# Eight small reorderings in one fused pair of transformer blocks: later side work, halves moved between transposings, loads behind a loop, tiles by k

## The chip, the cores and the metric

One core of one Trainium2 chip runs the whole program. The metric is the device time of one execution in microseconds (us), lower is better. The engines are TensorE (PE, its weight loads PEld), VectorE (DVE), ScalarE (ACT), GpSimd (POOL) and SyncE (SP), which here only issues DMA loads.

## What is computed

A hybrid block (layer norm, a gated delta rule beside stick-breaking attention, gates, an output projection, a mixture of experts) and then a second block of two layers (attention with rotary positions and a squared-ReLU MLP, then a pooling mixer and another MLP). 256 tokens plus 16 meta tokens, width 1024, all tensors float32. Cut to what matters:

```python
proj = h @ w_in                                     # 1024 -> qkv, z, beta, alpha, sb_qkv, gates
o_dn = gated_delta_rule_chunked(l2_normalize(q) * 128 ** -0.5, l2_normalize(k), v, beta, g)
o_dn = rms_norm(o_dn, dn_norm_g) * silu(dn_z)
o_sb = stick_breaking_attention(sq, sk, sv)
merged = gate0 * (o_dn @ w_branch_dn) + gate1 * (o_sb @ w_branch_sb)
h = layer_norm(alpha * h + merged @ w_out)
ffn = hierarchical_moe(h)                           # 4 groups x 8 experts, 2 experts per token
x = layer_norm(alpha * h + ffn)
...
x = x + moba_attention(rms_norm_2(x), w_qkv, w_o, cos, sin)
x = x + squared_relu_mlp(rms_norm_2(x), w_up, w_down)
x = x + pool_mixer(rms_norm_2(x), w_groups, ls_scale)
x = x + squared_relu_mlp(rms_norm_2(x), w_up, w_down)
return rms_norm_2(x, norm_final)
```

## The kernel before, in words

**Halves.** Dense weights come in chunks of 1 MB (`wraw`), two halves of 128x1024 each. ACT casts a half to a rounded high part (L324), DVE subtracts that from the original to get the low part (L326, tile `wsplit`), and PE does three matmuls per product: high by high, low by high, high by low (L374, L375, L376 in `ws_half`, L412 to L414 in `xs_half`). So a half costs 24 matmuls of 256 columns or 12 of 512, and it can't go on without DVE's subtract. Halves are prepared ahead in four slots, and five raw chunks fit the ring. In the wide form (`ws_wide`, L385 and L386) tokens are split too, and one 512-column and one 256-column matmul per k does it.

**Order.** The kernel is written engine by engine through a framework that schedules each engine's queue when the program is built. `tc.issue_after(x)` puts an instruction behind `x` in its queue's order, without a wait. `wpost.after = (a, b)` does that to the cast (a) and the subtract (b) of the next halves of the second block's stream. Every engine runs its queue strictly in that order.

**Stages**, with the lines that the change touches:

- *First block's middle.* Three generators are stepped in turn: the delta rule (`delta`, its matrix inversions step by step, and a reciprocal root `rq` of the query norms, L811 and L812, made of the ten small DVE operations L437 to L446), the projections, and two stick-breaking attentions (L909 to L940). In the round with `it == 2` `router_weights` (L994 to L998) scales the router's matrix.
- *Branches.* For each of two token tiles c, DVE multiplies `oraw` by a gate (L1069) and PE transposes it (L1072). `BS_AT` says which of the four halves of the second branch's matrix run behind which transposing: (0, 1, 1) is one half behind c = 0, none behind c = 1, and three at the end. L957 evacuates them.
- *Experts.* 99 chunks of 1 MB (`wexp`) stream through; PE multiplies 32-row groups (L1460 is the down product). In the last group a loop `For_i` over overflowing experts runs `n_x` times, which is zero times here, but every engine passes its ends (L1551). Behind it stand the last down product, its scaling (`ysf`, L1555 on ACT, L1556 on DVE) and eight adding matmuls (L1559). The loop's spare weights use one buffer that `slot()` gives, and two loads of the second block (`wraw`) are issued by SP ahead of the loop. Then 32 filler matmuls (L507) run until the layer norm (L470, L471, L1578 to L1585) is through and PE transposes `h` (L1610); ACT and DVE make the tokens `xx` of the second block (L1614, L1616).
- *Second block's projections.* Six column groups n, each in four halves k0 = 0, 2, 4, 6; the first two run as `xs_front` (L424). POOL sums the squares (L1636, L1644, L1646) and `rstd_columns` has PE sum them over partitions (L1659) at n = 0, k0 = 6. `rope_rows` scales a group's rows (L1690), turns them (L1696), and PE transposes them (L1705) at k0 = 2 of the next group.
- *MLPs.* Four products of up tiles per group through `ws_wide`, then down (L1831 to L1833). The tokens come one k at a time (L1597, L1598).
- *Pool mixer.* The last down product feeds `last`: per token tile c a root (L454 to L461 on DVE) scales the pooling matrix, on DVE for c = 0 (L1893), on ACT for c = 1 (L1891). PE multiplies by it (L1908, then L1910 and L1911), and the result meets the mixer's weights.

Of the kernel before, what the change touches and what calls it, by code (L numbers as in the profile page):

```python
# [19 lines left out]
SEQ = 256  # L20
# [4 lines left out]
NG = 8  # L25
CAP = 32
LATE = 8
RS_AT = 6
FILL_SPEC = "0123"
# [19 lines left out]
G_ELSE = (1, 4, 6)  # L49
BS_AT = (0, 1, 1)  # L50
COUNT_AT = 0
DN_STEPS = (3, 5, 10, 11, 11)
DN_FILL = (7, 9)
# [229 lines left out]
def tile_hybrid_block(ctx: ExitStack, tc: tile.TileContext, A, out, dump=None, stop=99):  # L283
# [95 lines left out]
    def ws_wide(stream, m, xx, fn, newbank):  # L379
# [7 lines left out]
        fn(m, p)  # L387

    def ws_front(stream, ms, xh, xl, width, fn, newbank):

# [13 lines left out]
    def xs_half(stream, k0, nk, xh, xl, banks, t0=0):  # L404

        wh, wl = stream.half()
        for k in (k0, k0 + 1):
            w1 = wh[:, (k - k0) * 512:(k - k0 + 1) * 512]
            w2 = wl[:, (k - k0) * 512:(k - k0 + 1) * 512]
            for c in range(2):  # L410
                tsl = slice(t0 + c * 128, t0 + c * 128 + 128)
                PE.matmul(banks[c], xh[:, k, tsl], w1, start=k == 0, stop=False)  # L412
                PE.matmul(banks[c], xh[:, k, tsl], w2, start=False, stop=False)  # L413
                PE.matmul(banks[c], xl[:, k, tsl], w1, start=False, stop=k == nk - 1)  # L414

# [273 lines left out]
    def delta():  # L689
# [120 lines left out]
        V.tensor_scalar(rq, pn[:, :8], 1e-6, None, op0=OP.add)  # L810
        rq = rsqrt(rq, (128, 8))  # L811
        V.tensor_scalar(rq, rq, float(128.0 ** -0.5), None, op0=OP.mult)  # L812

# [13 lines left out]
        XTs = [None] * 3  # L827
        live = [0, 1, 2]
        while live:
            for i in list(live):  # L830
                r = next(gens[i])
                if r is not None:
                    XTs[i] = r
                    live.remove(i)
            yield
# [216 lines left out]
    while m_on or f_on or sticks:  # L1052
        if it == 2:
            router_weights()
# [342 lines left out]
    def overflow(wx):  # L1397
# [4 lines left out]
        def weights(i):  # L1402
            t = wx[:, i % 2 * 1024:i % 2 * 1024 + 1024]
            spare_weights(t, eg, ej, 2 * i, 2)
            return t
# [35 lines left out]
    def scatter(g, n, Pm, ys):  # L1441

        for c in range(2):
            for i in range(2):
                added[0] = PE.matmul(ya[c][n], Pm[:, c * 128:(c + 1) * 128], ys[i], start=g == 0 and i == 0,
                                     stop=g == NG - 1 and i == 1)

# [20 lines left out]
    for g in range(NG):  # L1468
# [72 lines left out]
        else:  # L1541
# [5 lines left out]

            wx = slot()
            with tc.issue_after(last_load[0].ins):
# [3 lines left out]
            down(py, full, hT, chunk(), 1)  # L1553
            ys = moe.tile([128, 512], F32, tag="xt", name="ysf")
            mark["ACT"] = S.activation(ys[:, :256], py[:, :256], AF.Copy, scale=Pw)  # L1555
            V.tensor_scalar(ys[:, 256:], py[:, 256:], Pw, None, op0=OP.mult)  # L1556
            for c in range(2):
                for q in range(2):
                    added[0] = PE.matmul(ya[c][1][:, hf[q]], Pm[:, c * 128:(c + 1) * 128].bitcast(F32), ys[:, hf[q]],  # L1559
                                         start=False, stop=q == 1)  # L1560
# [200 lines left out]
    for n in range(6):  # L1761
        pb = [bank2(), bank2()]
        for k0 in range(0, 8, 2):
            if n or k0 > 2:
                xs_half(wpost, k0, 8, xh, xl, pb)
            elif k0 == 2:
                xs_front(wpost, 2, 8, xh, xl, pb)
            if n == 0 and k0 == RS_AT:
                rs[:] = rstd_columns(acc)
            if k0 == 2:  # L1770
                for f in later:
                    f()
                later = []
            heads(n, k0)
        if n < 4:
            later.append(rope_rows(n, pb))
# [26 lines left out]
    def mlp(xx, acc, n_last, after):  # L1803
# [5 lines left out]
        def up(g):  # L1809
# [14 lines left out]

            for m in range(4):
                ws_wide(wpost, m, xx, fn, bank2)
# [59 lines left out]
    def last(c, n, o):  # L1886
        square_sum(c, n, o, ss)
        if n:
# [3 lines left out]
            else:  # L1892
                V.tensor_scalar(pmat[:, :, :144], pmat[:, :, :144], r, None, op0=OP.mult)  # L1893

# [32 lines left out]
    for q in range(2):  # L1927
        wh, wl = wpost.half()
        for j in range(4):
            m = 4 * q + j  # L1930
# [54 lines left out]
```

## Time and profile before

| | before |
|---|---|
| median of 3 runs | 1011.24 us (1010.31 to 1011.78) |
| the profiled execution's own time | 1012.06 us |
| its span | 1010.3 us |
| mean granted TensorE clock | 0.979 |
| busy PE, DVE, ACT, POOL | 944.3, 603.7, 483.4, 68.3 us |
| read from memory | 225.29 MB |

A row of the timeline gives start, duration, engine, line, operation, out<-in, shapes and count, and in brackets how long the engine was idle just before and what released it. Matmuls are pipelined, so a matmul's duration is longer than the distance to the next start; costs of many are taken by that distance. In a table by stretches "PEclk" is the granted clock: 1.00 is 2.4 GHz, 0.50 is 1.2 GHz, and numbers between mean that both occurred in the stretch.

### The profile page before, as it was taken

The page shows a single profiled execution, that of the slowest core. Times are in us where ns is not written, and L with a number is a line of the kernel's source. Part 1 is how long each engine was busy: PE and PEld are TensorE (multiplying, and loading weights), DVE is VectorE, ACT ScalarE, POOL GpSimd, SP SyncE. Part 2 cuts the span into 40 slices and gives each one's busy share as a digit, 9 for nine tenths or more (in the row PEclk, how much of TensorE's full clock was granted, in tenths as well). Part 3 has the DMA queues.
Part 4 walks back from the last instruction along what each step waited for, and adds up shares of the span by engine and source line. Part 5 has one row for each costly group of instructions (what it writes and reads, how often), then busy time and mean ns, then how long its engine had stood idle before and what let it go on. Part 6 is the DMA issues. An engine that isn't in the chain of part 4 may idle for free.

```text
span 1010.3 us, 14882 instructions
## 1 busy us (share of the span) xinstructions
PE 944.3 (93%) x5905; PEld 757.5 (75%) x5905; DVE 603.7 (60%) x1163; ACT 483.4 (48%) x846; POOL 68.3 (7%) x60
## 2 busy tenths in 40 slices
PE   6997999989999999987789999999999999999996
PEld 5996997989884534442368889888888788888885
DVE  7887564664863312231186777756666686666664
ACT  4855576434432111101155565755555576555552
POOL 0004232000300000000020001000000020000002
PEclk9999999999999999999989999999999999999999
DMA  9440223649689999999865434555555525555521
GB/s 363 165 165 1 90 84 121 249 187 355 249 315 406 416 425 423 426 423 426 352 236 179 167 126 176 180 174 201 180 195 182 193 84 209 184 191 182 193 84 42
DMA packets 34231, 227.32 MB, mean 225 GB/s; under 512 B 3936, under 2 KB 4704, under 8 KB 7664
## 3 DMA queue, kind: packets, MB, share of 16 engines
q1 hardware_dynamic: 34160, 226.36, 58.8%
q8 instruction: 47, 0.77, 0.3%
q14 instruction: 24, 0.20, 0.1%
HBM read 225.29 MB, written 1.05 MB: 224 GB/s over the span
## 4 chain that ended last, share of the span: by engine, by line
PE 72%; DMA 16%; DVE 6%; ACT 3%; POOL 2%; issue 1%; SPq 0%; POOLq 0%; ACTq 0%; DVEq 0%
DMA wexp<-in_wexp_dram 14%; PE bank L385 11%; PE bank L386 6%; PE acc L1831 6%; PE acc L1832 6%; PE acc L1833 6%; PE bank L375 5%; PE bank L376 5%; PE bank L374 5%; PE bank L413 3%; PE bank L414 3%; PE bank L412 3%; DMA wraw<-in_wpost_dram 2%; PE bank L1486 1%; DVE wsplit L326 1%; PE bank L674 1%
## 5 line engine op out<-in xcount | busy, mean ns | idle before, releaser
L326 DVE TENSOR_TENSOR wsplit<-wraw,wsplit 128x1024 fp32r<-128x1024 f32 x222 | 277.7, 1251 | 143.5 <-ACT wsplit L324 139.5
L324 ACT CAST wsplit<-wraw 128x1024 fp32r<-128x1024 f32 x222 | 233.0, 1051 | 144.8 <-PE acc L1833 79.7
L385 PE MATMUL bank<-xx,wsplit 128*128 128x512 f32 x512 | 179.0, 393 | 2.2 <-DVE xx L1598 2.2
L386 PE MATMUL bank<-xx,wsplit 128*128 128x256 f32 x512 | 142.8, 280 | 0.7 <-DVE wsplit L326 0.7
L385 PEld LDWEIGHTS bank<-xx,wsplit 128*128 128x128 f32 x512 | 96.1, 188 | 24.4 <-DVE xx L1598 3.5
L1831 PE MATMUL acc<-wsplit,mhh 128*128 128x512 f32 x256 | 100.5, 393 | 0.0
L1832 PE MATMUL acc<-wsplit,mhh 128*128 128x512 f32 x256 | 99.8, 390 | 0.0
L1833 PE MATMUL acc<-wsplit,mhl 128*128 128x512 f32 x256 | 99.7, 390 | 0.0
L386 PEld LDWEIGHTS bank<-xx,wsplit 128*128 128x128 f32 x512 | 96.2, 188 | 1.6 <-DVE wsplit L326 1.0
L375 PE MATMUL bank<-hh,wsplit 128*128 128x256 f32 (+1 forms) x304 | 88.4, 291 | 2.7 <-DVE wsplit L326 2.7
L374 PE MATMUL bank<-hh,wsplit 128*128 128x256 f32 (+1 forms) x304 | 89.6, 295 | 0.0
L376 PE MATMUL bank<-hl,wsplit 128*128 128x256 f32 (+1 forms) x304 | 87.7, 289 | 0.0
L1486 PE MATMUL bank<-wexp,xt 128*32 128x512 f32 x512 | 62.8, 599 | 5.3 <-DMA wexp<-in_wexp_dram 4.3
L375 PEld LDWEIGHTS bank<-hh,wsplit 128*128 128x128 f32 x304 | 58.6, 193 | 3.6 <-DVE wsplit L326 3.2
L374 PEld LDWEIGHTS bank<-hh,wsplit 128*128 128x128 f32 x304 | 58.7, 193 | 0.4 <-issue 0.2
L376 PEld LDWEIGHTS bank<-hl,wsplit 128*128 128x128 f32 x304 | 58.7, 193 | 0.0
L1833 PEld LDWEIGHTS acc<-wsplit,mhl 128*128 128x128 f32 x256 | 48.1, 188 | 10.1
L1832 PEld LDWEIGHTS acc<-wsplit,mhh 128*128 128x128 f32 x256 | 48.1, 188 | 9.9 <-DVE wsplit L326 0.3
L1831 PEld LDWEIGHTS acc<-wsplit,mhh 128*128 128x128 f32 x256 | 48.1, 188 | 9.7
L1816 ACT COPY relu<-bank 128x256 f32<-128x256 f32 x64 | 23.8, 373 | 62.8 <-PE bank L386 62.7
L1512 ACT ACTIVATE hid<-bank 128x256 f32<-128x256 f32 x8 | 3.1, 383 | 89.1 <-PE bank L1486 89.1
L1460 PE MATMUL bank<-wexp,hT 128*32 128x512 f32 x256 | 32.6, 624 | 9.8 <-DMA wexp<-in_wexp_dram 4.2
(542 smaller groups left out, 1648.8 us busy)
## 6 DMA issues: line engine op xcount, KB each, us to landing
wexp<-in_wexp_dram SPq DMA_DIRECT2D x99, 1024.0 KB, 19.6
wraw<-in_wpost_dram SPq DMA_DIRECT2D x81, 1024.0 KB, 4.7
wraw<-in_wpre_dram SPq DMA_DIRECT2D x30, 1024.0 KB, 4.9
h<-in_x_dram SPq DMA_DIRECT2D x2, 512.0 KB, 4.4
eb<-in_rowv_dram SPq DMA_DIRECT2D x2, 512.0 KB, 10.7
out_dram<-of SPq DMA_DIRECT2D x4, 256.0 KB, 2.1
cpre<-in_cst_dram SPq DMA_DIRECT2D x1, 915.5 KB, 10.3
pmat<-in_poolm_dram SPq DMA_DIRECT2D x1, 544.0 KB, 3.2
```

Source lines behind the costliest of these rows:

```text
L324: S.copy(hi, src)
L326: (sub or V).tensor_tensor(lo, src, hi.bitcast(F32), op=OP.subtract)
L374: PE.matmul(p[:, :width], wh[:, o:o + 128], xh[:, k, :], start=k == 0, stop=False)
L375: PE.matmul(p[:, :width], wl[:, o:o + 128], xh[:, k, :], start=False, stop=False)
L376: PE.matmul(p[:, :width], wh[:, o:o + 128], xl[:, k, :], start=False, stop=k == nk - 1)
L385: PE.matmul(p, wh[:, o], xx[:, k].rearrange("p q t -> p (q t)"), start=k == 0, stop=False)
L386: PE.matmul(p[:, :SEQ], wl[:, o], xx[:, k, 0], start=False, stop=k == 7)
L1460: behind[0] = PE.matmul(py[32 * e:32 * e + 32, sl], hT[:, i, 32 * e:32 * e + 32], w[:, e, sl], start=i == 0, stop=i == 1).ins
L1486: behind[0] = PE.matmul(pg[32 * e:32 * e + 32, :], xt[:, k, 32 * e:32 * e + 32], w[:, e, :], start=k == 0, stop=k == 7).ins
L1831: PE.matmul(ac[c][n], hh_, wh, start=g == 0 and k == 0, stop=False)
L1832: PE.matmul(ac[c][n], hh_, wl, start=False, stop=False)
L1833: PE.matmul(ac[c][n], hl_, wh, start=False, stop=g == 7 and k == 3)
```

## The change

The root `rq` is computed in the fourth round of the inversions, behind a mark in DVE's queue, and the router's weights in round 7. `BS_AT` becomes (0, 3, 3): three halves between the two transposings, one behind. The overflow loop takes its buffers from the weight ring, and the scaled rows behind the loop get two tiles, each for its own half; one 128x1 matmul per token tile closes the first half of the sums. The sums of squares are taken by PE at n = 1, behind the first half of that group, the first group's rotation comes after it, and its transposings at k0 = 4. The first two up tiles of both MLPs run by k, each k for both tiles (`wide_front`). The pooling matrix's first scaling becomes the mark behind which the subtracts of the next halves are put. Lines below line 50 move up by 1 to 26 numbers in the changed file (L326 becomes L327, L1893 L1918).

```diff
-RS_AT = 6
...
-BS_AT = (0, 1, 1)
+BS_AT = (0, 3, 3)
+ROUTER_AT = 7
+RQ_AT = 4
...
+    def wide_front(stream, ms, xx, fn, newbank):
+        ws = [stream.half() for _ in ms]
+        ps_ = [newbank() for _ in ms]
+        for k in range(8):
+            o = slice(k * 128, k * 128 + 128)
+            for (wh, wl), p in zip(ws, ps_):
+                PE.matmul(p, wh[:, o], xx[:, k].rearrange("p q t -> p (q t)"), start=k == 0, stop=False)
+                PE.matmul(p[:, :SEQ], wl[:, o], xx[:, k, 0], start=False, stop=k == 7)
+        for m, p in zip(ms, ps_):
+            fn(m, p)
...
-        rq = rsqrt(rq, (128, 8))
-        V.tensor_scalar(rq, rq, float(128.0 ** -0.5), None, op0=OP.mult)
...
         while live:
+            n_live += 1
+            if n_live == RQ_AT:
+                with tc.issue_after(mark["DVE"].ins):
+                    rq = rsqrt(rq, (128, 8))
+                    V.tensor_scalar(rq, rq, float(128.0 ** -0.5), None, op0=OP.mult)
...
-        if it == 2:
+        if it == ROUTER_AT:
             router_weights()
...
-            wx = slot()
+            wx = [ring.tile([128, 2048], F32, tag="w", name="wexp") for _ in range(N_RING)]
...
-            ys = moe.tile([128, 512], F32, tag="xt", name="ysf")
-            mark["ACT"] = S.activation(ys[:, :256], py[:, :256], AF.Copy, scale=Pw)
-            V.tensor_scalar(ys[:, 256:], py[:, 256:], Pw, None, op0=OP.mult)
+            ys = [moe.tile([128, 256], F32, tag="hT", name="ysf"), moe.tile([128, 256], F32, tag="xt", name="ysf")]
+            V.tensor_scalar(ys[0], py[:, :256], Pw, None, op0=OP.mult)
+            mark["ACT"] = S.activation(ys[1], py[:, 256:], AF.Copy, scale=Pw)
             for c in range(2):
+                PE.matmul(ya[c][0][:, 0:1], ident, C("strict")[:, 0:1], start=False, stop=True)
...
-            if n == 0 and k0 == RS_AT:
-                rs[:] = rstd_columns(acc)
-            if k0 == 2:
+            if n == 1 and k0 == 0:
+                with tc.issue_after(last_of[0].ins):
+                    rs[:] = rstd_columns(acc)
+                later.append(rope_rows(0, first_pb))
+            if k0 == (4 if n == 1 else 2):
...
-            for m in range(4):
+            if g == 0:
+                wide_front(wpost, (0, 1), xx, fn, bank2)
+            for m in range(2 if g == 0 else 0, 4):
                 ws_wide(wpost, m, xx, fn, bank2)
...
-                V.tensor_scalar(pmat[:, :, :144], pmat[:, :, :144], r, None, op0=OP.mult)
+                wpost.after = (None, V.tensor_scalar(pmat[:, :, :144], pmat[:, :, :144], r, None, op0=OP.mult))
```

Three places in the queues. First DVE's queue in the first block's middle, before, up to the subtract (L326) of the half that the projections use next; L927 are the stick-breaking scans, `rs_t` and `rs_y` belong to the root `rq`, `rcb` and `wrt` to the router's weights:

```order
L927 SCALAR_TENSOR_TENSOR sbwork<-sbwork 128x272
L443 TENSOR_TENSOR rs_t<-rs_t,rq 128x8
L995 TENSOR_REDUCE rcb<-bank 128x36
L444 TENSOR_SCALAR rs_y<-rs_t 128x8
L996 TENSOR_SCALAR rcb<-rcb 128x36
L997 TENSOR_TENSOR rcb<-rcb,cpre 128x36
L445 TENSOR_TENSOR rs_y<-rs_y,rs_t 128x8
L998 TENSOR_TENSOR wrt<-wr_1111,rcb 128x288
L446 SCALAR_TENSOR_TENSOR rs_y<-rs_y,rs_z 128x8
L326 TENSOR_TENSOR wsplit<-wraw,wsplit 128x1024
```

and changed, from the scan of 832 columns (L923, now L941), with which the same piece begins, on:

```order
L941 SCALAR_TENSOR_TENSOR sbwork<-sbwork 128x832
L327 TENSOR_TENSOR wsplit<-wraw,wsplit 128x1024
L945 SCALAR_TENSOR_TENSOR sbwork<-sbwork 128x144
L945 SCALAR_TENSOR_TENSOR sbwork<-sbwork 128x272
L945 SCALAR_TENSOR_TENSOR sbwork<-sbwork 128x144
L945 SCALAR_TENSOR_TENSOR sbwork<-sbwork 128x272
L327 TENSOR_TENSOR wsplit<-wraw,wsplit 128x1024
L958 COPY sbwork<-bank 16x512
L327 TENSOR_TENSOR wsplit<-wraw,wsplit 128x1024
L936 SCALAR_TENSOR_TENSOR sbwork<-bank,cpre 128x416 x2
```

That subtract (now L327) stands ahead of the four scans; the root and the router's tiles are gone from here.

Second, PE's queue in the second block's projections, before, at the sum over partitions (L1659). `wsplit_4716` is the fourth half of group 0, `wsplit_4781` the first of group 1:

```order
L412 MATMUL bank_4741<-wsplit_4716,xx_4660 128x512
L412 MATMUL bank_4742<-wsplit_4716,xx_4660 128x512
L1659 MATMUL bank_4800<-cst_73,acc1_4798 128x1 x2
L412 MATMUL bank_4847<-wsplit_4781,xx_4660 128x512
L413 MATMUL bank_4741<-wsplit_4716,xx_4660 128x512
L414 MATMUL bank_4741<-wsplit_4716,xx_4660 128x512
L413 MATMUL bank_4742<-wsplit_4716,xx_4660 128x512
```

and changed, where `wsplit_4723` and `wsplit_4788` are those two halves, and the sum over partitions (L1678 now) follows 22 matmuls behind the first two rows:

```order
L425 MATMUL bank_4748<-wsplit_4723,xx_4667 128x512
L425 MATMUL bank_4749<-wsplit_4723,xx_4667 128x512
L425 MATMUL bank_4803<-wsplit_4788,xx_4667 128x512
L426 MATMUL bank_4803<-wsplit_4788,xx_4667 128x512
L427 MATMUL bank_4803<-wsplit_4788,xx_4667 128x512
L425 MATMUL bank_4804<-wsplit_4788,xx_4667 128x512
L426 MATMUL bank_4804<-wsplit_4788,xx_4667 128x512
L426 MATMUL bank_4748<-wsplit_4723,xx_4667 128x512
L427 MATMUL bank_4748<-wsplit_4723,xx_4667 128x512
```

The sum is gone from the place behind the first two matmuls of the fourth half, and five matmuls of the next group stand there, ahead of the first one (L426) that reads the fourth half's low part.

Third, DVE's queue at the pooling matrix, before, from its scaling for c = 0 (L1893) to the end of the root for c = 1 (L461), which ACT's scaling waits for:

```order
L1893 TENSOR_SCALAR pmat<-pmat,r_7205 128x4x144
L456 SCALAR_TENSOR_TENSOR r_7240<-r_7238,rst 128x1
L457 SCALAR_TENSOR_TENSOR r_7239<-r_7240,r_7238 128x1
L458 SCALAR_TENSOR_TENSOR r_7240<-r_7239,rst 128x1
L459 TENSOR_SCALAR r_7238<-r_7240 128x1
L460 TENSOR_TENSOR r_7238<-r_7238,r_7240 128x1
L461 SCALAR_TENSOR_TENSOR r_7238<-r_7238,r_7239 128x1
L326 TENSOR_TENSOR wsplit<-wraw,wsplit 128x1024
```

and changed, the same piece (L1918 to L476):

```order
L1918 TENSOR_SCALAR pmat<-pmat,r_7212 128x4x144
L471 SCALAR_TENSOR_TENSOR r_7247<-r_7245,rst 128x1
L327 TENSOR_TENSOR wsplit<-wraw,wsplit 128x1024
L472 SCALAR_TENSOR_TENSOR r_7246<-r_7247,r_7245 128x1
L473 SCALAR_TENSOR_TENSOR r_7247<-r_7246,rst 128x1
L327 TENSOR_TENSOR wsplit<-wraw,wsplit 128x1024
L474 TENSOR_SCALAR r_7245<-r_7247 128x1
L475 TENSOR_TENSOR r_7245<-r_7245,r_7247 128x1
L476 SCALAR_TENSOR_TENSOR r_7245<-r_7245,r_7246 128x1
```

Two subtracts stand inside the root for c = 1: one stood behind it, the other far ahead of it, in front of the piece shown.

SP's queue loses the two `wraw` loads ahead of the loop and has all six behind it; the load of `causal` (192 KB, L1682), which stood behind those, is ahead of the loop now.

## Rows read from the trace of the kernel before

**Rows 1.** The page: shares of the chain that ended last, by engine

```profile
PE 72%; DMA 16%; DVE 6%; ACT 3%; POOL 2%; issue 1%; SPq 0%; POOLq 0%; ACTq 0%; DVEq 0%
```

**Rows 2.** Stretches: PE, PEld, DVE, ACT, POOL busy, PEclk, DMA share, GB/s

```profile
101.00:104.00 3.00, 3.00 (x13) 3.00 (x14) 1.25 (x3) 0.00 (x0) 0.00 (x0) 0.50 0.64 224
105.00:210.00 105.00, 102.78 (x822) 93.89 (x821) 64.81 (x105) 61.94 (x106) 22.70 (x13) 1.00 0.36 131
217.00:220.00 3.00, 2.61 (x13) 2.64 (x14) 0.94 (x2) 0.59 (x1) 0.00 (x0) 0.50 0.99 421
227.00:303.00 76.00, 73.73 (x512) 66.63 (x511) 47.62 (x112) 31.32 (x45) 8.65 (x8) 0.98 0.80 307
303.00:499.00 196.00, 176.83 (x1238) 80.50 (x1237) 50.60 (x139) 31.23 (x64) 0.00 (x0) 0.98 1.01 420
500.00:507.00 7.00, 5.12 (x16) 4.40 (x17) 3.23 (x8) 1.99 (x2) 0.00 (x0) 0.51 0.61 226
524.00:530.00 6.00, 4.77 (x13) 3.99 (x14) 4.91 (x17) 0.00 (x0) 1.17 (x1) 0.50 0.73 269
808.00:812.00 4.00, 3.50 (x30) 3.45 (x31) 2.65 (x8) 2.84 (x5) 0.00 (x0) 1.00 0.02 2
```

**Rows 3.** Timeline of DVE, first block's middle

```profile
99.68 1.21 DVE L326 TENSOR_TENSOR wsplit<-wraw,wsplit 128x1024 fp32r<-128x1024 f32 x1
```

**Rows 4.** Timeline of PE at the router's matmuls and its longest wait

```profile
85.33 1.13 PE L994 MATMUL bank<-wr,cst 128*128 128x288 f32 x4
...
89.61 0.63 PE L652 MATMUL bank<-cst,XT 128*128 128x128 f32 x4 [2.51 <-DVE XT L656]
```

**Rows 5.** Timeline of PE, the half that waits

```profile
96.53 0.37 PE L374 MATMUL bank<-hh,wsplit 128*128 128x272 f32 x1
...
100.95 0.59 PE L375 MATMUL bank<-hh,wsplit 128*128 128x272 f32 x1 [2.06 <-DVE wsplit L326]
...
105.37 0.38 PE L936 MATMUL bank<-cst,sbwork 128*128 128x128 f32 x2
```

**Rows 6.** Timeline of PE between the last transposings and behind

```profile
209.07 0.60 PE L1072 MATMUL bank<-cst,oraw 128*128 128x128 f32 x4
...
217.39 1.09 PE L1072 MATMUL bank<-cst,oraw 128*128 128x128 f32 x4 [4.87 <-DVE oraw L1069]
...
227.69 0.28 PE L374 MATMUL bank<-hh,wsplit 128*128 128x256 f32 x1
```

**Rows 7.** Chain of waits around the loop: start, us, what

```profile
481.12 20.29 DMA wraw<-in_wpost_dram
...
501.88 3.78 PE acc L1559 x8
...
510.57 0.57 ACT xx L1614
```

**Rows 8.** The page: the second block's loads, us from issue to landing

```profile
wraw<-in_wpost_dram SPq DMA_DIRECT2D x81, 1024.0 KB, 4.7
```

**Rows 9.** Timeline, all engines, projections of the second block

```profile
519.76 1.21 DVE L326 TENSOR_TENSOR wsplit<-wraw,wsplit 128x1024 fp32r<-128x1024 f32 x1
...
522.18 1.33 POOL L1644 TENSOR_TENSOR acc<-acc,sq 128x512 f32<-128x512 f32 x1
522.31 3.94 DVE L326 TENSOR_TENSOR wsplit<-wraw,wsplit 128x1024 fp32r<-128x1024 f32 x2
...
525.23 1.01 PE L1659 MATMUL bank<-cst,acc 128*128 128x1 f32 x4 [3.73 <-POOL acc L1646]
```

**Rows 10.** Waits of PE, projections to first layer's end

```profile
PE bank L385 <- DVE xx L1598: 0.9, 1, 0.9
```

**Rows 11.** Waits of PE, pool mixer and last MLP's start

```profile
PE bank L385 <- DVE xx L1598: 1.4, 3, 0.8
```

**Rows 12.** Timeline, all engines, pooling matrix

```profile
808.50 2.05 PE L1908 MATMUL bank<-pmat,rows 128*128 128x128 f32 x16 [1.56 <-DVE pmat L1893]
...
809.63 0.73 ACT L1891 ACTIVATE pmat<-pmat,r 128x512 f32<-128x512 f32 x1
```

More of the change, by code (lines that the diff above doesn't have):

```diff
@@ L413, in xs_half @@
                 PE.matmul(banks[c], xh[:, k, tsl], w2, start=False, stop=False)
-                PE.matmul(banks[c], xl[:, k, tsl], w1, start=False, stop=k == nk - 1)
+                last_of[0] = PE.matmul(banks[c], xl[:, k, tsl], w1, start=False, stop=k == nk - 1)
+    last_of = [None]
     def xs_front(stream, n, nk, xh, xl, banks):
@@ L827, in delta @@
         XTs = [None] * 3
-        live = [0, 1, 2]
+        live, n_live = [0, 1, 2], 0
         while live:
+            n_live += 1
[3 more added lines that the diff above has]
+                    V.tensor_scalar(rq, rq, float(128.0 ** -0.5), None, op0=OP.mult)
             for i in list(live):
@@ L1402, in weights @@
         def weights(i):
-            t = wx[:, i % 2 * 1024:i % 2 * 1024 + 1024]
+            t = wx[i % N_RING][:, :1024]
             spare_weights(t, eg, ej, 2 * i, 2)
@@ L1445, in scatter @@
                 added[0] = PE.matmul(ya[c][n], Pm[:, c * 128:(c + 1) * 128], ys[i], start=g == 0 and i == 0,
-                                     stop=g == NG - 1 and i == 1)
+                                     stop=False)
     def warm_after(n):
@@ L1553, in tile_hybrid_block @@
             down(py, full, hT, chunk(), 1)
-            ys = moe.tile([128, 512], F32, tag="xt", name="ysf")
-            mark["ACT"] = S.activation(ys[:, :256], py[:, :256], AF.Copy, scale=Pw)
-            V.tensor_scalar(ys[:, 256:], py[:, 256:], Pw, None, op0=OP.mult)
+            ys = [moe.tile([128, 256], F32, tag="hT", name="ysf"), moe.tile([128, 256], F32, tag="xt", name="ysf")]
+            V.tensor_scalar(ys[0], py[:, :256], Pw, None, op0=OP.mult)
+            mark["ACT"] = S.activation(ys[1], py[:, 256:], AF.Copy, scale=Pw)
             for c in range(2):
+                PE.matmul(ya[c][0][:, 0:1], ident, C("strict")[:, 0:1], start=False, stop=True)
                 for q in range(2):
-                    added[0] = PE.matmul(ya[c][1][:, hf[q]], Pm[:, c * 128:(c + 1) * 128].bitcast(F32), ys[:, hf[q]],
+                    added[0] = PE.matmul(ya[c][1][:, hf[q]], Pm[:, c * 128:(c + 1) * 128].bitcast(F32), ys[q],
                                          start=False, stop=q == 1)
@@ L1774, in tile_hybrid_block @@
             heads(n, k0)
-        if n < 4:
+        if n == 0:
+            first_pb = pb
+        elif n < 4:
             later.append(rope_rows(n, pb))
@@ L1928, in tile_hybrid_block @@
         wh, wl = wpost.half()
+        wpost.after = (None, None)
         for j in range(4):
```

## The prediction

> **What bounds the kernel now.** I read the page's chain first: PE makes 72% of it, DMA 16% [rows 1], so time is won only where PE stands still or runs at the low clock on that chain, or where the expert stream ends earlier. Then the table by stretches: from 105 to 210 PE is busy 102.78 of 105 us, from 303 to 499 the loads move 420 GB/s at a DMA share of 1.01 and PE is busy 176.83 of 196, and in four short stretches (101, 217, 500 and 524 us) the granted clock is 0.50 or 0.51, the 1.2 GHz level [rows 2]. Each of the four lies behind a stop of PE: 2.06 us for a subtract [rows 5], 4.87 us for the gated rows [rows 6], the loop's end [rows 7], 3.73 us for POOL's sum [rows 9]. Shorter stops (1.6 us at the pooling matrix, 0.9 at the first MLP) are there too [rows 10, 12]. The change touches each of these places, so I go through them in order of time. The sum is made against the profiled execution, 1012.06 us, which is 0.8 over the median of the runs; I take 0.8 off at the end.
>
> **1. Root and router, -4.8.** PE starts a half at 96.53 and can't go on to its second matmul before the low part: the subtract runs 99.68 to 100.89 because the root's and the router's operations stand ahead of it, and the half's last matmul gives way to the next work only at 105.37, much of it at the 1.2 GHz level [rows 2, 3, 5]. In the changed queue that subtract stands ahead of the scans, long before 96. The half is 24 matmuls of 272 columns; 272 columns at 2.4 GHz are 0.113 us, with a little for the start 0.125 each, 3.0 in all: done at 99.6 instead of 105.37, which is 5.8 saved. What is moved must be paid: the router's four matmuls (1.13 us) stood just ahead of a 2.51 us stop of PE, so they were free [rows 4]; they now stand in a stretch where PE is full, which costs 1.0. The DVE operations of both go where DVE waits; DVE is busy 64.81 of 105 us there [rows 2], so they cost nothing unless they land in front of a subtract, at most one of 1.2. Bounds: -3.5 and -5.8. PE stays full up to 210, so the shift arrives there.
>
> **2. Three halves between the transposings, -5.2.** Before, one half runs behind the first transposing, PE stops 4.87 us until 217.39, and the other three run behind the second, the first of them at the low clock, until 227.69 [rows 2, 6]. A half is 24 matmuls of 256 columns at 0.117, 2.8 us. Now three run from 209.4 to 217.9. DVE's gated rows, ready at about 217.3 before, are later: three evacuations of 256 columns stand in that chain now (a quarter of a subtract's columns, 0.3 to 0.4 each), of which two wait for PE, and one subtract of 1.2 [rows 3]; I get 219.1. So PE still waits 1.2, transposes (0.4; before 0.60 with its tail) and runs the fourth half: 222.5 instead of 227.7. The stop of 1.56 at 807 left the clock at 1.00 [rows 2, 12], so I expect no fall. Bounds: -4.4 (another subtract in that chain) and -5.8 (no wait).
>
> Both gains, 10.0, must pass the experts. Before the stream is full (227 to 303) the loads move 307 GB/s and PE is busy 73.73 of 76 us [rows 2]: there the loads wait for buffers that PE and DVE free, so the stream's start moves with PE, and its end with its start.
>
> **3. Loop, -2.4.** Before, two loads of the next block are issued ahead of the loop, the second at 481.12; it lands 20.29 us later, behind the last experts, and only then does the chain go on with the adding matmuls at 501.88 [rows 7]. Two loads of 1.05 MB at 420 GB/s are 5.0 us of the stream, so without them the last load lands about 496.5 and the loop lets go when PE, ACT and DVE are through, about 499.5: 2.4 saved. PE's shorter stop could also keep the clock: 3.78 us for eight adding matmuls is at the 1.2 GHz level [rows 2, 7], half of that is 1.9. Against it the loads start at 499.4: the first lands 4.7 later by the page's median [rows 8], 504.1, where before it had landed before 501.5. The casts of its two halves then stand in ACT's queue beside the layer norm's output, and the second of them delays `xx`, by 1.2 if a cast is taken to be no longer than its subtract [rows 3]. The new 128x1 matmuls and the halves of the scaled rows, which wait for each other in turn, are given 0.7. Together -2.4 -1.9 +1.2 +0.7 = -2.4 with the clock kept; the bounds are -4.3 (nothing of the costs) and -0.5 (the clock falls as before).
>
> **4. Later scale, -3.6.** PE stands still from 521.5 to 525.23, then runs at the 1.2 GHz level to about 530 [rows 2, 9]; 4.8 us of busy time at half speed are 2.4 lost, so the place costs 6.1. In the changed queue PE first has five matmuls of the next half, whose low part is ready at 521.0 [rows 9]; at 0.22 each they last until 522.6. Then it needs the fourth half's low part: two subtracts last 3.94 together from 522.31 [rows 9], the first until about 524.3. So 1.7 of stop is left, and the rotation behind the later sum, with a subtract of 1.2 inside it, makes PE wait some 0.8 at the transposings (estimate; 0 to 1.5). 6.1 less 2.5 is 3.6. If the clock falls at the 1.7, 2.4 is given back: -1.2. A single subtract lasts 1.21 just before; here two last 3.94, beside POOL's adds [rows 9]. Were the first one 1.21 too, it would end at 523.5 and the gain be 4.4, my upper bound. The Trainium skill, GPSIMD Engine Reference, section Specifications, says that GpSimd's SBUF interfaces are shared with VectorE and that VectorE instructions with two SBUF inputs contend there. The trace agrees, 3.94 against twice 1.21, and since the changed queues leave POOL's adds beside these subtracts, by the rule the gain is 3.6 and not 4.4.
>
> **5. Two up tiles by k, -0.5.** At the first MLP PE waits 0.9 for tokens [rows 10]; two tiles per k take twice as long per token, so it goes: -0.9. At the second MLP PE waits 1.4 in three pieces [rows 11], and already finds other tiles' work between; in the fixed order it waits for the late tokens in line instead: +0.4, from 0 to +1.7 with a fall of the clock.
>
> **6. Pooling matrix, +3.3.** This works against the change. The edit is to keep subtracts out of the first scaling's way, but the subtract that moves stood in free time, and the one inside the first root stays. In the changed queue two subtracts of 1.2 stand inside the root for c = 1, between the first scaling and the end. Before, ACT's scaling starts at 809.63 and PE, which starts on c = 0 at 808.50, needs its result (0.73 later) at 810.4 without waiting [rows 12]. Two times 1.2 later, ACT starts at 812.0 and PE waits 2.4. It comes right behind a stop of 1.56 [rows 12]. A stop of 2.06 behind such another ended at the 1.2 GHz level at 101 us [rows 2, 5], so I expect a fall here, some 0.9 of it on the path, since DVE and ACT limit the mixer behind. Bounds: +2.4 (clock kept) and +3.9.
>
> **Sum:** -4.8 -5.2 -2.4 -3.6 -0.5 +3.3 = -13.2; 1012.06 - 13.2 = 998.9, and **998.0** against the median. All bounds at their ends give 992.4 and 1006.3.
>
> **Rivals.**
> - *PE's clock falls at the loop and at the later sum as before.* Stops of 2 to 4 us remain at both; for it speak the falls behind 2.06 and 3.73 [rows 5, 9], against it that 1.56 alone did not bring one [rows 2, 12]. Terms 3 and 4 become -0.5 and -1.2: 1002.3. Chance 0.2.
> - *The early gains don't pass the experts*, since the stream of 420 GB/s is the bound from 303 to 499 and would end when it ended [rows 2]. Against it: 307 GB/s before 303, so it isn't yet bound by the memory there. 10.0 are lost: 1008. Chance 0.1.
> - *Slower: the six loads behind the loop share the engines* and land together instead of one after the other. At the 226 GB/s of 500 to 507 [rows 2], 6.3 MB take 28 us, and the first projection, due at about 509, would start at 529: 1018. The point from which it decides: the first half is needed at 509, so its chunk at 507; slower than before it is when the chunk lands 13 us after that, at 520, some 20 after issue. For it speaks that a load has taken 20.29 in a full queue [rows 7], against it that 81 of them have a median of 4.7 [rows 8]. Chance 0.04. The Trainium skill, DMA: Bandwidth & Descriptors, section Queues, rings and completion order, has each engine take descriptors in ring order, by which the first chunk lands first; no run here shows six loads issued at once on idle engines.
> - *The moved root and router land ahead of other subtracts and the scheduled order puts the waits back elsewhere*, so that nothing is left beyond noise: 1010 to 1013. Chance 0.04; PE's idle places are named and the orders differ there, which speaks against it.
>
> **How the numbers follow.** Forecast 0.58, the clock 0.2, the stream 0.1, the loads 0.04, nothing 0.04, better than my bounds 0.04. The range 992 to 1006 holds the forecast with its bounds and the clock's rival, about 0.8. A measurement of this kernel can tell 0.2%, 2 us, from no change. Faster: all but two, 0.92; same 0.04; slower 0.04.
>
> **What would show it.** Term 1: no stop at 97 to 101 and no 0.50 there. Term 2: the second transposing behind a stop of about 1 us, the gates starting 10 us earlier than 227.69. Term 3: the adding matmuls no longer behind a `wraw`, some 2.4 earlier than the shift alone. Term 4: no stop for POOL's sum, one of 1 to 2 us for a subtract. Term 6: a stop of 2 us or more ahead of L1910's successor, with ACT's scaling behind two subtracts. I am wrong if the gates start earlier and the stream doesn't end earlier, if the first half of the second block comes later than `xx`, or if term 6 is near zero.

## The result, and the profile after

The change makes the kernel faster by 1.1%: a median of **999.75 us** (998.62 to 1000.64, 4 runs) against 1011.34 (4 runs), a ratio of 0.9886 with a 95% interval of 0.9873 to 0.9898. Forecast were 998.0 us and a range of 992 to 1006. The profiled execution took 998.62 us with a span of 996.8, against 1012.06 and 1010.3 before: 13.4 us, where the sum said 13.2. The sum came out better than its terms did, as the table shows. The table gives, for one PE instruction that both kernels have at the place, its start before and its start after; a step of the shift from one line to the next is what that stretch gained or lost.

| place on PE (line before) | before | after | shift | step | forecast |
|---|---|---|---|---|---|
| first of the last transposings (L1072) | 209.07 | 203.74 | 5.33 | +5.33 | +4.8 (term 1) |
| gates (L374 on `hh`) | 227.69 | 217.08 | 10.61 | +5.28 | +5.2 (term 2) |
| behind the router (L1195) | 296.48 | 284.53 | 11.95 | +1.34 | 0 |
| last down half (L1460) | 496.60 | 485.35 | 11.25 | -0.70 | 0 |
| first projection, second block (L424) | 511.60 | 498.59 | 13.01 | +1.76 | +2.4 (term 3) |
| behind the projections (L1715) | 560.56 | 543.09 | 17.47 | +4.46 | +3.6 (term 4) |
| first MLP's down (L1831) | 649.35 | 630.73 | 18.62 | +1.15 | +0.9 (term 5) |
| first pooling product (L1908) | 808.50 | 789.91 | 18.59 | -0.03 | 0 |
| mixer's end (L1937) | 819.61 | 806.25 | 13.36 | -5.23 | -3.3 (term 6) |
| last down (L1831) | 1000.70 | 987.24 | 13.46 | +0.10 | -0.4 (term 5) |

Two steps of the table hold time that no edit won. Where the half of term 1 starts, at 96.53 before [rows 5] and 95.89 after, the changed kernel is already 0.64 ahead: it won that within the first 30 us, where no edit acts. So term 1 itself is worth 4.7. And the +1.34 at the router comes from a clock that fell there in the execution before (last section).

The stretches of the changed kernel, with the columns of [rows 2]:

```profile
96.00:99.00 3.00, 3.00 (x26) 3.00 (x25) 1.90 (x1) 2.83 (x4) 3.00 (x2) 1.00 0.11 44
105.00:210.00 105.00, 102.86 (x817) 94.34 (x817) 69.66 (x128) 60.58 (x108) 22.08 (x13) 1.00 0.37 136
213.00:217.00 4.00, 3.24 (x28) 3.27 (x29) 3.19 (x6) 1.55 (x2) 0.00 (x0) 1.00 0.77 283
277.00:285.00 8.00, 7.85 (x71) 7.66 (x69) 6.42 (x47) 4.03 (x7) 0.00 (x0) 1.00 0.97 380
303.00:485.00 182.00, 163.98 (x1130) 73.32 (x1131) 43.77 (x103) 26.90 (x57) 0.00 (x0) 0.98 1.00 418
488.00:491.00 3.00, 2.89 (x9) 2.49 (x10) 1.26 (x2) 0.00 (x0) 0.00 (x0) 0.56 0.69 218
511.00:518.00 7.00, 6.99 (x32) 5.81 (x33) 6.97 (x13) 2.11 (x2) 2.70 (x2) 1.00 0.85 328
784.00:795.00 11.00, 7.57 (x54) 6.65 (x53) 8.18 (x25) 6.78 (x16) 0.00 (x0) 1.00 0.26 85
795.00:800.00 5.00, 5.00 (x28) 5.00 (x28) 2.39 (x6) 2.76 (x7) 0.00 (x0) 0.56 0.62 236
800.00:804.00 4.00, 4.00 (x27) 4.00 (x27) 3.23 (x8) 1.43 (x4) 0.00 (x0) 0.70 0.01 2
```

Of the four places of [rows 2] at the 1.2 GHz level, three are at 1.00 now (96, 213 and 511 us); the loop's stays at 0.56, and a new one is at 795, behind the pooling matrix. The page's chain now reaches back from the end only to the loop, at 487.71 us, so its shares are not comparable with [rows 1].

The timeline of PE at the first block's three places, where [rows 5] and [rows 6] had stops of 2.06 and 4.87:

```profile
95.89 0.37 PE L375 MATMUL bank<-hh,wsplit 128*128 128x272 f32 x1
...
99.00 0.49 PE L954 MATMUL bank<-cst,sbwork 128*128 128x128 f32 x3
...
203.74 0.60 PE L1090 MATMUL bank<-cst,oraw 128*128 128x128 f32 x4
...
213.76 0.63 PE L1090 MATMUL bank<-cst,oraw 128*128 128x128 f32 x4 [0.88 <-DVE oraw L1087]
...
217.08 0.28 PE L375 MATMUL bank<-hh,wsplit 128*128 128x256 f32 x1
```

The half that hung until 105.37 starts at 95.89 and makes way for the next work at 99.00, with no stop inside. The second transposing waits 0.88 (forecast 1.2), and the gates start 13.3 us behind the first one, where it was 18.6.

The timeline of all engines at the loop, for [rows 7]:

```profile
488.11 0.38 PE L1576 MATMUL acc<-cst 128*128 128x1 f32 x2 [1.70 <-ACTq L1569]
488.36 2.04 PE L1578 MATMUL acc<-ysf,Pm 128*128 128x256 f32 x4
...
490.48 1.75 PE L1578 MATMUL acc<-ysf,Pm 128*128 128x256 f32 x4
...
494.17 1.04 ACT L325 CAST wsplit<-wraw 128x1024 fp32r<-128x1024 f32 x1 [6.70 <-DMA wraw<-in_wpost_dram]
...
496.52 1.97 PE L1629 MATMUL bank<-cst,h 128*128 128x128 f32 x16 [0.71 <-ACT h L1603]
497.02 1.04 ACT L325 CAST wsplit<-wraw 128x1024 fp32r<-128x1024 f32 x1
497.96 1.94 ACT L1633 ACTIVATE xx<-bank,gb 128x256 fp32r<-128x256 f32 x4
...
500.01 3.36 PE L439 MATMUL bank<-wsplit,xx 128*128 128x512 f32 x12 [0.69 <-DVE xx L1635]
```

The adding matmuls no longer wait for a load: they start 13.5 us earlier, 2.3 more than the last down half did. They still take 3.79 us (2.04 and 1.75), against 3.78 before, since the clock fell here all the same. The first chunk, issued at 487.90, is cast at 494.17; the second cast (497.02) stands ahead of `xx` (497.96).

The timeline at the projections, for [rows 9]:

```profile
509.37 0.63 ACT L1650 ACTIVATE sq<-x 128x512 f32<-128x512 f32 x1
...
509.74 6.25 DVE L327 TENSOR_TENSOR wsplit<-wraw,wsplit 128x1024 fp32r<-128x1024 f32 x4
...
510.14 1.96 POOL L1663 TENSOR_TENSOR acc<-acc,sq 128x512 f32<-128x512 f32 x1 [0.61 <-ACT sq L1650]
511.01 0.19 PEld L426 LDWEIGHTS bank<-wsplit,xx 128*128 128x128 f32 x1 [1.41 <-DVE wsplit L327]
511.01 0.50 PE L426 MATMUL bank<-wsplit,xx 128*128 128x512 f32 x1 [0.98 <-DVE wsplit L327]
```

PE's stop of 3.73 is one of 0.98, for the subtract that starts at 509.74. It starts 0.40 ahead of POOL's add (510.14), and by the chain it takes 1.22, while the add takes 1.96. Before it was the other way round: the add started 0.13 ahead of the subtract and took 1.33, and two subtracts took 3.94 [rows 9]. Of the other three subtracts of the group two run beside POOL's sums, and they are stretched to 2.30 and 1.75. The rotation behind the later sum made PE wait nowhere.

The timeline at the pooling matrix, for [rows 12]:

```profile
789.34 0.52 DVE L1918 TENSOR_SCALAR pmat<-pmat,r 128x576 f32<-128x576 f32 x1
...
789.90 1.22 DVE L327 TENSOR_TENSOR wsplit<-wraw,wsplit 128x1024 fp32r<-128x1024 f32 x1
...
789.91 2.05 PE L1933 MATMUL bank<-pmat,rows 128*128 128x128 f32 x16 [1.56 <-DVE pmat L1918]
...
791.36 1.22 DVE L327 TENSOR_TENSOR wsplit<-wraw,wsplit 128x1024 fp32r<-128x1024 f32 x1
...
793.07 0.72 ACT L1916 ACTIVATE pmat<-pmat,r 128x512 f32<-128x512 f32 x1 [1.91 <-DVE r L476]
...
793.84 0.49 PE L1935 MATMUL bank<-pmat,rows 128*128 128x128 f32 x2 [1.88 <-ACT pmat L1916]
...
795.51 0.37 PE L1936 MATMUL bank<-pmat,rows 128*128 128x16 f32 x2
795.72 0.78 PE L1935 MATMUL bank<-pmat,rows 128*128 128x128 f32 x2
```

Two subtracts stand inside the root, as read from the queue, ACT's scaling comes late, and PE stops 1.88 us behind its stop of 1.56. It starts again at the 2.4 GHz level; at about 795.6 the clock falls, and a pair of matmuls that took 0.49 takes 0.78.

PE's waits in the first and second MLP, for [rows 10] and [rows 11]: the first has none for `xx` left, and this is the second:

```profile
PE bank L397 <- DVE xx L1617: 1.2, 2, 1.0
PE bank L387 <- DVE wsplit L327: 1.0, 1, 1.0
```

### The profile page after: what moved, and what is told of

Read it like the earlier page. It is cut to its first block, busy times and chain, and to the rows that moved or that the text cites. A ratio compares the mean times of both kernels' runs of the same rounds, so it can differ in the third digit from the quotient of the medians.

```text
span 996.8 us, 14894 instructions
## 1 busy us (share of the span) xinstructions
PE 940.0 (94%) x5909; PEld 753.4 (76%) x5909; DVE 601.3 (60%) x1163; ACT 483.1 (48%) x846; POOL 69.4 (7%) x60
## 4 chain that ended last, share of the span: by engine, by line
PE 46%; DVE 3%; ACT 1%; issue 0%; POOL 0%; ACTq 0%; DVEq 0%
PE bank L386 11%; PE acc L1856 6%; PE bank L387 6%; PE acc L1857 6%; PE acc L1858 6%; PE bank L427 2%; PE bank L426 2%; PE bank L425 2%; DVE wsplit L327 1%; PE bank L375 1%; PE bank L376 1%; PE bank L377 1%; PE bank L397 0%; PE bank L439 0%; PE bank L1935 0%
## 5 line engine op out<-in xcount | busy, mean ns | idle before, releaser
L327 DVE TENSOR_TENSOR wsplit<-wraw,wsplit 128x1024 fp32r<-128x1024 f32 x222 | 277.5, 1251 | 136.7 <-ACT wsplit L325 134.4
L386 PE MATMUL bank<-xx,wsplit 128*128 128x512 f32 x480 | 167.2, 392 | 0.0
L387 PE MATMUL bank<-xx,wsplit 128*128 128x256 f32 x480 | 134.3, 280 | 1.0 <-DVE wsplit L327 1.0
L386 PEld LDWEIGHTS bank<-xx,wsplit 128*128 128x128 f32 x480 | 90.1, 188 | 19.8
L387 PEld LDWEIGHTS bank<-xx,wsplit 128*128 128x128 f32 x480 | 90.2, 188 | 1.9 <-DVE wsplit L327 1.3
```

The source lines that it names most:

```text
L327: (sub or V).tensor_tensor(lo, src, hi.bitcast(F32), op=OP.subtract)
L386: PE.matmul(p, wh[:, o], xx[:, k].rearrange("p q t -> p (q t)"), start=k == 0, stop=False)
L387: PE.matmul(p[:, :SEQ], wl[:, o], xx[:, k, 0], start=False, stop=k == 7)
```

## The experiments

Each part alone, on the kernel before or taken out of the changed one. Medians are of 5 or more runs, ratios against runs of the kernel before on the same chip; shifts are read as in the table, against the profiled execution before.

**The changed kernel without the part at the pooling matrix**

```diff
-                wpost.after = (None, V.tensor_scalar(pmat[:, :, :144], pmat[:, :, :144], r, None, op0=OP.mult))
+                V.tensor_scalar(pmat[:, :, :144], pmat[:, :, :144], r, None, op0=OP.mult)
...
-        wpost.after = (None, None)
```

> The changed kernel with the pooling matrix's part undone, all else as changed. My theory: in the changed trace PE's lead over the kernel before shrinks from 18.6 us at the start of the pooling matmuls to 13.4 at the mixer's end; 1.9 of that is the wait for ACT's scaling behind two subtracts, the rest the 1.2 GHz level that follows it. So without the part 5.2 come back: about 994.5 us, PE's wait for ACT's scaling is gone and the clock stays at 1.00 through the mixer. Rival: the low clock there comes by chance and not from this wait; then only 1.9 to 2.4 come back: about 997.5.

Measured: **993.64 us** (990.9 to 995.43), ratio 0.9823 (0.9805 to 0.9842), the fastest of all. The shift is 18.42 at the first pooling product and 18.42 at the mixer's end. Its timeline at the scaling for c = 1:

```profile
791.22 0.72 ACT L1916 ACTIVATE pmat<-pmat,r 128x512 f32<-128x512 f32 x1
...
792.00 0.49 PE L1935 MATMUL bank<-pmat,rows 128*128 128x128 f32 x2
```

And its stretches in the mixer, behind the start of the second product, with the columns of [rows 2]:

```profile
794.00:798.00 4.00, 4.00 (x36) 4.00 (x36) 3.56 (x10) 3.33 (x8) 0.00 (x0) 1.00 0.57 233
798.00:802.00 4.00, 4.00 (x34) 3.91 (x33) 3.29 (x9) 3.47 (x8) 0.00 (x0) 1.00 0.01 2
```

With no subtract inside the root, PE goes on without a stop at 792.00 and the clock stays at 1.00. PE is full here at the 2.4 GHz level too, so whatever the clock takes away in the mixer is lost. Term 6 has the sign that was forecast.

**That part alone**, the edit above the other way round on the kernel before.

> The kernel before with the pooling matrix's part alone. My theory: one stop of about 1.9 us more at the second scaling and a clock at 0.50 behind it for some 6 us, together 5.2 lost: 1016.5 us. Rival (the prediction's lower bound): a stop of 2.4 and the clock kept, 1013.7. Second rival: the subtracts land differently without the other parts and nothing changes, 1011.3.

Measured: 1016.29 us (1014.74 to 1017.04), ratio 1.0047 (1.0034 to 1.006), so slower. From first pooling product to mixer's end the shift goes from 0.86 to -4.36, which is -5.22: the same price as in the joined change. Its stretches:

```profile
810.00:814.00 4.00, 2.43 (x20) 2.43 (x20) 1.17 (x5) 1.63 (x4) 0.00 (x0) 0.93 0.90 336
814.00:816.00 2.00, 2.00 (x12) 2.00 (x11) 1.12 (x3) 1.15 (x4) 0.00 (x0) 0.50 0.82 344
816.00:820.00 4.00, 4.00 (x20) 4.00 (x20) 2.68 (x7) 1.91 (x5) 0.00 (x0) 0.50 0.02 4
```

PE is busy throughout at the 1.2 GHz level from 814 to 820, as it is at the 2.4 GHz level without the part: it is PE that limits the mixer, not DVE and ACT. Of the 5.2, 2.0 are lost by the start of the second product (shift -1.15), with the stop, and 3.2 behind it, with the fall.

**Without that part, and with the second half's subtract behind the root** (the root's last operation is kept in `root[0]`):

```diff
+        root[0] = V.scalar_tensor_tensor(y, y, RS_Q[2], z, op0=OP.add, op1=OP.mult)
...
     for q in range(2):
+        if q:
+            wpost.after = (None, root[0])
         wh, wl = wpost.half()
```

> The changed kernel, with the pooling part in another way: the subtract that stands inside the first token tile's root (the first half of the second MLP) is put behind the second tile's root, the other subtracts where they stood before. My theory: the first scaling comes 1.2 us earlier, the stop of 1.56 ahead of it shrinks to 0.3 to 0.4, and the second scaling follows in time: 994.5 less 1.0 to 1.2, about 993.3 us. Rival: ACT's cast stands ahead of its scaling and holds the second one where it was, so PE waits there what it won before: 994.5.

Measured: 994.91 us (992.33 to 998.04), ratio 0.9835 (0.9814 to 0.9856), not to be told from the version without this edit. Its timeline at the pooling matrix:

```profile
790.35 2.05 PE L1935 MATMUL bank<-pmat,rows 128*128 128x128 f32 x16 [0.55 <-DVE pmat L1920]
...
791.53 1.07 ACT L325 CAST wsplit<-wraw 128x1024 fp32r<-128x1024 f32 x1
...
792.48 0.74 ACT L1918 ACTIVATE pmat<-pmat,r 128x512 f32<-128x512 f32 x1
...
793.27 0.49 PE L1937 MATMUL bank<-pmat,rows 128*128 128x128 f32 x2 [0.87 <-ACT pmat L1918]
```

The stop of 1.56 shrinks to 0.55, as meant. But ACT's queue now has a cast (791.53) ahead of its scaling, and what PE won at the first product it lost at the second, where it waits 0.87. With the subtract out of the way, the cast is what the second scaling waits behind, as the rival had it.

**Without that part, and with fillers between the last down half and the adding matmuls**, to keep the clock at the loop (`warm` issues matmuls whose result nobody reads; `warm(12)` shows as 24 in the trace):

```diff
             down(py, full, hT, chunk(), 1)
+            with tc.issue_after(behind[0]):
+                warm(12)
```

> The changed kernel with the pooling part undone and 12 filler matmuls more (some 1.4 us of PE work that nothing reads) behind the last down product at the loop. My theory: the clock falls at the loop because PE stands still for 1.7 us; filled, it stays at 1.00, the eight adding matmuls take about 1.9 instead of 3.8, and the time falls by 1.5 to 1.9 against the kernel with the pooling part undone: about 993 us. Rival: the clock falls there whatever stands in the gap, as it fell at 292 us in the kernel before although PE was busy throughout: no change, 994.5.

Measured: 998.19 us (994.55 to 1000.87), ratio 0.9861 (0.9839 to 0.9883). The edit missed its place, as PE's timeline shows:

```profile
490.03 4.55 PE L522 MATMUL bank<-cst 128*128 128x128 f32 x24
494.42 1.03 PE L1580 MATMUL acc<-ysf,Pm 128*128 128x256 f32 x4
```

The fillers came behind the loop, between the 128x1 matmuls and the adding ones, and put these off by 4.4 us. PE's stop ahead of them stayed (1.79), and the clock fell behind it as without the fillers, which themselves ran mostly at the 1.2 GHz level: 24 in 4.55 us. The adding matmuls then ran at the 2.4 GHz level (1.03). What a filled gap would give stays open.

**The root alone**

```diff
-        rq = rsqrt(rq, (128, 8))
...
+            if n_live == 4:
+                with tc.issue_after(mark["DVE"].ins):
+                    rq = rsqrt(rq, (128, 8))
```

> The kernel before with the later root of the query norms alone; the router's weights stay in round 2. My theory: the root's ten small DVE operations were the larger part of what stood ahead of the awaited subtract, but the router's four remain there, so PE still waits, by a shorter stop than 2.06 us, and the clock may fall as before: 1 to 4 us gained, 1007.5 to 1010. Rival: the scheduler puts the subtract ahead of the scans with either part gone, and the whole 5 to 6 are won: about 1005.5.

**The router weights alone**

```diff
-        if it == 2:
+        if it == 7:
             router_weights()
```

> The kernel before with the router's weights in round 7 alone; the root stays. My theory: the root is what holds the subtract, so most of the stop at 97 to 101 us stays, the router's four matmuls cost 1 us in a full stretch, and the time is within 2 us of before, 1010 to 1012. Rival: the router's four operations were the ones that mattered, 1006 to 1008.

Measured: 1006.05 us for the root alone (ratio 0.995, 0.9935 to 0.9966) and 1006.48 for the router alone (0.9955, 0.9939 to 0.9971). At the first transposing the shifts are 5.55 and 4.45, against 5.33 with both; less what each execution was ahead at the start of the half (0.56, 0.25 and 0.64), the edits won 5.0, 4.2 and 4.7. Either part alone brings nearly all of term 1, and they don't add. DVE's subtract, at 99.68 before [rows 3], stands in DVE's timeline of the root alone at:

```profile
95.56 1.21 DVE L326 TENSOR_TENSOR wsplit<-wraw,wsplit 128x1024 fp32r<-128x1024 f32 x1
```

and in that of the router alone at:

```profile
91.57 1.21 DVE L326 TENSOR_TENSOR wsplit<-wraw,wsplit 128x1024 fp32r<-128x1024 f32 x1
```

It has to be through when PE's second matmul is due, some 0.2 us behind the half's start (96.53 before). Each edit alone lets the schedule put it there or nearly so: with the root alone PE still waits 0.49 for it. Both expectations were wrong (the root alone was to win a part only, the router alone next to nothing), and both rivals came true.

**Three halves between the transposings, alone**

```diff
-BS_AT = (0, 1, 1)
+BS_AT = (0, 3, 3)
```

> The kernel before with three branch halves between the last two transposings alone. My theory: PE's stop of 4.87 us falls to about 0.9 to 1.2, the clock doesn't fall behind it, the gates start 5.2 earlier and the expert stream starts and ends that much earlier too: 1006.1 us, or 1005 if the clock also stays up at the router, where it fell at 292 us before. Rival: the stream of the experts' weights ends when it ended before, so nothing is left: 1011.3.

Measured: 1005.96 us, ratio 0.9948 (0.9932 to 0.9964). The shift is 0.03 at the first transposing, 5.32 at the gates and 5.16 at the last down half: the gain arrives, and it passes the expert stream whole.

**The loop's part alone** (its lines of the diff, from `wx` to the 128x1 matmuls):

> The kernel before with the loop's buffers from the ring alone, so that all loads of the second block stand behind the loop. My theory: the adding matmuls start 2.3 to 2.5 earlier, the clock still falls behind the loop, and the second cast delays the first tokens by 0.75: 1.4 to 1.7 gained, about 1009.8 us. Rival (the prediction): the clock is kept and 2.4 or more are gained, 1008.9 or less. Second rival: the first loads land too late for the first half: slower than 1011.3.

Measured: 1006.73 us, ratio 0.9961 (0.9947 to 0.9975). The timeline of PE behind the loop:

```profile
499.47 0.38 PE L1558 MATMUL acc<-cst 128*128 128x1 f32 x2 [1.70 <-ACTq L1551]
499.72 1.11 PE L1560 MATMUL acc<-ysf,Pm 128*128 128x256 f32 x4
```

The stop is the same 1.70 as in the joined change, but the clock stayed, against the expectation: the adding matmuls take twice 1.11. The shift is -0.10 at the last down half, 2.16 at the adding matmuls, 3.10 at the first projection, and 6.00 behind the projections. The last 2.9 were not forecast: the schedule orders the projections otherwise here too, and PE waits 2.14 for a subtract at 520.91 and then 0.27 for POOL's sum, in place of 3.73, with the clock at 1.00. So the parts at the loop and at the later scale overlap.

**The later scale alone** (`last_of`, `first_pb` and the condition on `k0`):

> The kernel before with the later scale alone. My theory: 4.5 to 5 us gained, 1006.4 to 1006.9, since the order of ACT's queue changes too: the last square stands behind a cast, so POOL's adds start later and the awaited subtract lasts 1.2 and not 2; PE stops about 1 us and the clock stays at 1.00. Rival (the prediction): the subtract stays slow beside POOL, PE stops 1.7 and waits 0.8 at the transposings: 3.6 gained, 1007.7.

Measured: 1008.62 us, ratio 0.998 (0.9967 to 0.9993). In the profiled execution the projections gain 3.84 (0.31 to 4.15). The timeline at the fourth half:

```profile
522.04 5.10 DVE L326 TENSOR_TENSOR wsplit<-wraw,wsplit 128x1024 fp32r<-128x1024 f32 x3
...
524.38 0.50 PE L413 MATMUL bank<-wsplit,xx 128*128 128x512 f32 x1 [2.10 <-DVE wsplit L326]
```

Here POOL's add starts first, at 521.91, and the awaited subtract lasts from 522.04 to about 524.3, as term 4 assumed; PE waits 2.10, and the clock stays at 1.00 behind it. In the joined change the same subtract started first and took 1.22. The expectation, that the later scale alone puts the add behind the subtract, was wrong; the prediction's case came true.

**The two up tiles by k, alone** (`wide_front` in the first group of both MLPs):

> The kernel before with the first two up tiles of both MLPs by k alone. My theory: the first MLP's wait of 0.9 us goes, the second MLP's three waits turn into others of the same sum: 0.9 to 1.1 gained, 1010.3 us, at the edge of what can be measured. Rival: the fixed order costs the second MLP more than the first wins: 1011 to 1013.

Measured: 1009.27 us, ratio 0.9985 (0.9976 to 0.9994). The first MLP gains 1.16 (2.24 to 3.40); the second changes by 0.05.

## Why the prediction was right, and where it was not

The time is 1.75 us from the forecast and inside the range. Two terms hit, and four were off. That the profiled executions are 13.4 us apart, where the sum said 13.2, is luck: 0.6 of it lies ahead of the first edit's place and 1.3 comes from the clock at the router. Without these it is 11.5, near the 11.6 between the medians. So the terms brought 1.7 less than forecast: term 6 cost 1.9 more, term 3 won 0.6 less and the expert stream lost 0.7, while terms 4 and 5 gave 0.9 and 0.8 more.

1. **Root and router: right** (+4.7 for +4.8, counted from the half's start). The mechanism is the forecast one: the half is through at 99.0, which with the 0.64 of the earlier start is the 99.6 that I had. The moved router costs what was forecast: the shift is 6.37 at that place and 5.33 at the first transposing, and most of the 1.0 between them goes where the router's matmuls stand now (122.27). The full PE carries the rest on. Not said was that either part alone does it.
2. **Three halves: right** (+5.3 for +5.2), the wait included (0.88 for 1.2), with the clock kept. The rival that the experts swallow it fell: 5.16 of 5.3 passed in the part alone, and in the joined change only 0.70 was lost over the stream.
3. **Loop: mis-sized, +1.8 for +2.4.** The step that failed is "PE's shorter stop could also keep the clock", +1.9: the clock fell behind the stop of 1.70 and the adding matmuls took 3.79. The exit was right (+2.3 for +2.4). The costs (-1.2 and -0.7) were too high: from the adding matmuls to the first projection 0.5 was lost, and the second wait for `xx`, 0.69, is counted in the next step. The clock fell behind this stop in four of the five executions whose kernel has this part (the joined change and the three made from it); only the part alone kept it. So at the loop the clock's rival was the likelier case.
4. **Later scale: mis-sized, +4.5 for +3.6**, a little above its upper bound of 4.4. The step that failed is the one from "the changed queues leave POOL's adds beside these subtracts" to a slow subtract: in the joined order ACT's last square (509.37) stands behind a cast, POOL's add starts at 510.14, and the subtract that PE awaits, which had started 0.40 ahead of it, takes its 1.22 all the same. The other price in that term, 0.8 at the transposings, was nothing. The Trainium skill, GPSIMD Engine Reference, section Specifications, says that VectorE instructions with two SBUF inputs contend with GpSimd. The traces agree, and they show who pays: the one that starts second. In the scale alone, where POOL's add has a start of 0.13, the awaited subtract takes 2.29 and the add 1.33; in the joined change it is 1.22 and 1.96. In the traces of all twelve kernels the 117 such subtracts that started ahead of a POOL operation beside them took 1.2 each, and those that started behind one took up to 2.3. What failed was not who runs beside whom, but who starts first.
5. **Wide tiles: mis-sized, +1.15 for +0.9** at the first MLP; the second, for which I had taken 0.4 off, lost nothing that shows.
6. **Pooling matrix: mis-sized, -5.2 for -3.3**, beyond its bound of 3.9. The sign and the two subtracts inside the root were right, and the stop nearly so (1.88 for 2.4). The step that failed is "some 0.9 of it on the path, since DVE and ACT limit the mixer behind": the fall costs 3.2, since PE is full there at the 2.4 GHz level too and no slack takes up the slower clock. The changed kernel's stretches give the same by an estimate: 5 us at 0.56 and 4 us at 0.70 are 3.4 lost. Both the joined change and the part alone show it.

Not in the sum: +0.6 from ahead of the first edit's place, +1.3 at the router, from a clock that fell in the execution before (below), and -0.7 over the stream, where the other executions lie between -0.6 and +0.4. **The rivals:** the clock fell at the loop and not at the later sum, so neither case is the whole truth; the gains passed the stream; the loads behind the loop came one after the other: the five issued from 487.90 to 489.96 land between 494.15 and 503.89, some 2.4 us apart, so the first is used 6.3 us behind its issue and not 20; and the waits that root and router caused did not come back elsewhere.

The version that leaves term 6 out beats both kernels: 993.64 us. The interval of its ratio, 0.9805 to 0.9842, lies wholly below that of the changed kernel.

## What to carry to other kernels

Read the queue of each engine at the place, and not the intent of the edit: the part meant to keep subtracts out of the way put two into a root that PE waits for, and was the one part that lost. Two edits that take away the same wait don't add, so try each alone before both are paid for. Before you price a fall of the clock, ask how full PE is behind it: in the mixer PE had no slack even at 2.4 GHz, so the whole fall was lost. When two engines contend, look at which starts first: the later one paid here.

## What was not expected of the hardware

The granted clock fell where PE had not stopped. In the kernel before, at the router of the first block, the stretches read:

```profile
286.00:292.00 6.00, 6.00 (x54) 5.87 (x53) 4.97 (x27) 2.05 (x4) 0.00 (x0) 0.99 0.95 384
292.00:295.00 3.00, 3.00 (x16) 3.00 (x16) 2.72 (x21) 2.56 (x4) 0.00 (x0) 0.50 0.99 369
```

PE is busy without a break, and yet the clock is 0.50 from 292 on. The changed kernel runs the same work at 1.00 (277 to 285 us, above), and so do six of the other executions, while four fell like the kernel before. Up to there the later scale alone (fell) and the loop's part, the pooling part and the wide tiles alone (all kept) have the same order on PE as the kernel before. In the seven that kept it, the way from the gates to the router is 1.29 to 1.35 us shorter than before, and no edit explains it. Nor does the length of a stop decide alone: 1.70 at the loop brought a fall in the joined change and none with the loop's part alone; 2.10 and 2.14 at the projections brought none; and at the pooling matrix the fall came 1.7 us after PE had started again. The executions also differ ahead of the places that the edits touch: the half of term 1 starts between 2.1 us later and 1.7 earlier than in the execution before. So a term that hangs on the clock is a chance of a price, and a single profile can be 1 to 2 us off by it. What decides it was not found.
